# One gate block is moved from the third group's chain to the last group of a hybrid Conformer and RWKV-7 layer, and the norm's row sums refer to four blocks

## The chip, the cores and the metric

The kernel runs on one core of one Trainium2 chip. The metric is the device time of one execution in microseconds (us); less is better. A profile is one execution, and its span runs from the first to the last instruction. PE is TensorE, DVE VectorE, ACT ScalarE, POOL GpSimd, SP SyncE, which here issues nearly all the transfers.

## The reference

One layer on 512 tokens of width 1024, all in float32. From the modulated norm `h` one wide product gives the columns of a convolution branch, of an RWKV-7 branch and of two gates:

```python
h = modulate(rms_norm(x, g_norm1), shift1, scale1)
u = h @ w_in
u_conv, u_rwkv, u_gate = jnp.split(u, [2 * CONV_DIM, 2 * CONV_DIM + RWKV_COLS], axis=-1)
y_conv = conformer_conv(u_conv, ...)   # z*sigmoid, 31 taps, layer_norm, silu, z @ w_pw + b_pw
y_rwkv = rwkv7_mix(u_rwkv, ...)        # 16 heads of 64, a recurrence over 512 tokens, @ w_o
g_conv, g_rwkv = jnp.split(jax.nn.sigmoid(u_gate), N_BRANCH, axis=-1)
merged = g_conv * y_conv + g_rwkv * y_rwkv
x = x + gate1[:, None, :] * (merged @ w_out)
h2 = modulate(rms_norm(x, g_norm2), shift2, scale2)
x = x + gate2[:, None, :] * (jnp.square(jax.nn.relu(h2 @ w_ff1)) @ w_ff2)
```

The gates have 2 x 1024 columns, that is 16 blocks of 128. They need only `h`, and their result is used only after both branches.

## The kernel before

Columns lie on partitions, tokens on the free axis, so a tile is 128 columns by 512 tokens. A dense product of one block of 128 output columns (`wload`, `wmul`, lines 211 to 231) loads 1024x128 weights by SP (512 KB), splits them on ACT into a rounded high part (line 215) and on POOL into the rest (line 216), and runs 3 x 8 matmuls of 128x512 (lines 223 to 225): high by high, high by low, low by high. Raw weights, high and low parts have two buffers each, so the weights of a block are made ready about two blocks ahead.

The RWKV branch goes in four groups of two column blocks (four heads). For a group: `group_k` (line 547) makes two key blocks (read by ACT at line 263) and the low-rank decay and rate; `group_prep` (593) makes two receptance and two value blocks and the pair products (line 664, masked by DVE at 667) of 8 chunks of 64 tokens; `group_solve` (705) inverts the triangular part on DVE in 62 small dependent steps (lines 722 and 724) between transposes (715, 730, 732); `group_solve2` (739) finishes this on PE (748, 754); `group_chain` (759) walks over the 8 chunks, each a chain of small matmuls with ACT and DVE between them; `group_post` (810) normalizes, and reads for each block a 64 KB weight g2t into a single buffer (833) for a product (835).

Blocks that depend on `h` alone fill PE beside this: six convolution blocks (`conv_in`, 514; the 31 taps are DVE steps at line 145; line 530 adds a block to the column sums `csum`) and the 16 gate blocks (`gate_in`, 848: the dense block, a sigmoid on ACT at line 850, a store at 851). `WINDOWS` says for each group which of them are traced ahead of its chain and, after the bar, behind it ("c" is a convolution block, "g" a gate block).

Instructions are traced in program order, and a scheduler orders each engine's queue from that: what is ready goes, by priority, which is the place in the program less an offset from the table `FORWARD`. `issue_after` and `amid` only add that an instruction stands behind a given other one on its engine. Each queue then runs strictly in its order on the chip.

The last group has the layer norm of the convolution in front of its chain (lines 888 to 909): mean by a matmul over `csum` (893), ACT's copy (895), eight tiles read back and the mean subtracted on POOL (903), squares on ACT (905), row sums on PE (`rms_rows`, 188), then root (198), reciprocal on DVE (199), a broadcast by PE (183) and a copy (909). The silu of the normed blocks (938 to 941) makes the input of the pointwise product `w_pw` (line 947), which then runs beside the last chain. The row sums of tile j are put behind a numbered matmul of the blocks just traced:

```python
steps = sum(dense_log[-lnb:], [])          # 24 matmuls of each of the last lnb blocks
with tc.issue_after(steps[min(NORM_AT + j * NORM_STEP, len(steps) - 1)].ins):   # 63, 9
    rms_rows(pq, sq, j == 0, j == KC - 1)
```

After the last chain's place in the program the rest of the gate blocks, the pointwise product, `w_o`, `w_out` and the feed-forward follow, all dense.

Of the kernel before, what the change touches and what calls it, by code (L numbers as in the profile page):

```python
# [19 lines left out]
NCH = 8  # L20
TAPS = 31

WINDOWS = ("ccgg|g", "ccggg|", "cc|gggg", "ggg|ggg")

FORWARD = {
    "k": (10, 10, 10, 10), "solve": (127, 153, 48, -153), "window": (0, 7, -47, -43), "chain": (-98, 348, 51, 37),
# [31 lines left out]
def tile_block(ctx: ExitStack, tc: tile.TileContext, xT, vec, cst, x0, w_ada, w_in, w2a2, g2w,  # L58
# [8 lines left out]
    def nm(s):  # L67
        cnt[0] += 1
        return f"{s}{cnt[0]}"

    @contextmanager
    def forward(section, g=0, shift=True):

        off = FORWARD[section][g]
        if not off:
            yield
            return
        with tc.high_priority(offset=off):
            a = tc.cur_priority
            yield  # L80
            n = tc.cur_priority - a
        if shift:
            tc.cur_priority += n
# [3 lines left out]
    def t2k(shape=(P, T), dt=F32, tag="t2k", bufs=9):  # L87
        home = sb if tag == "t2k" else pools["A2" if tag in A2 else "A"]
        return home.tile(list(shape), dt, name=nm(tag), tag=tag, bufs=bufs)
# [10 lines left out]
    def pmisc(shape=(P, T), name="misc"):  # L100
        return psum("misc", 2, shape, name)
# [83 lines left out]
    def rms_rows(pq, sq, start, stop):  # L185

        for q in range(4):
            pe.matmul(pq[32 * q:32 * q + 32, :], ones[:, 0:32], sq[:, q * P:(q + 1) * P], start=start, stop=stop,
                      tile_position=(0, 32 * q))
# [6 lines left out]
    def rms_tail(pq, ei):  # L196
        rt = sb.tile([P, P], F32, name=nm("nrm"), tag="nrm", bufs=1)
        act.activation(rt, pq, AF.Sqrt, scale=1.0 / D, bias=eps[:, ei:ei + 1])
        dve.reciprocal(rt, rt)
        pr = pmisc((P, T), "rmsb")  # L200
        bcast_rows(pr, rt)
        return pr
# [30 lines left out]
    def after_dense():  # L233

        return tc.issue_after(last[0].ins)

    @contextmanager
    def amid(n, d=-1):

        with forward("amid", shift=False), tc.issue_after(dense_log[d][n].ins):  # L240
            yield
# [455 lines left out]
    def group_bonus(g, G, b):  # L697
        rH, rL, v = G.bonus[b]
        pb = pmisc(name="bonus")
        pe.matmul(pb, blkr, rH, start=True, stop=False)  # L700
        pe.matmul(pb, blkr, rL, start=False, stop=True)
        dve.tensor_tensor(v, pb, v, ALU.mult)
        nc.sync.dma_start(vb_d[g * NB + b], v)

    def group_solve(G):


        U = NB * NCH
        AD = atile("s4", (P, 2, NB, NCH, 32), 2)
        for q in range(4):  # L710
            d, e = q % 2, 1 - q // 2
            for h in range(2):
                act.copy(AD[32 * q:32 * q + 32, h], G.G[32 * q:32 * q + 32, :, e, :, 32 * d:32 * d + 32])
        AT = atile("s4", (P, 32, 32), 2)
        dve.transpose(AT, AD.rearrange("p h b c t -> p t (h b c)"))
        X = psum("Y", 1, (P, 32, 16))
        act.copy(X, xi)
        tmp = atile("tm", (P, 144))
        for s in range(31):
            n, w = 31 - s, s // 2 + 1  # L720
            tv = tmp[:, 0:n * w].rearrange("p (t c) -> p t c", c=w)
            dve.tensor_tensor(tv, AT[:, s + 1:32, s].unsqueeze(2).to_broadcast([P, n, w]),  # L722
                              X[:, s, 0:w].unsqueeze(1).to_broadcast([P, n, w]), ALU.mult)
            dve.tensor_tensor(X[:, s + 1:32, 0:w], tv, X[:, s + 1:32, 0:w], ALU.add)  # L724
        Xf = atile("s4", (P, 32, 16, 2), 2)
        act.copy(Xf[:, :, :, 0], X)
        dve.stream_shuffle(Xf[:, :, :, 1], Xf[:, :, :, 0], [(i + 16) % 32 for i in range(32)])
        Xv = Xf.rearrange("p t c h -> p t (c h)")
        T1 = atile("s4", (P, 32, 32), 2)
        dve.transpose(T1.rearrange("p u c -> p c u"), Xv.rearrange("p t c -> p c t"))  # L730
        TT = atile("TT", (P, 32, 32))
        G.solved = dve.transpose(TT.rearrange("p u t -> p t u"), Xv)
        for q in range(4):
            d, e = q % 2, 1 - q // 2
            act.copy(G.G[32 * q:32 * q + 32, :, e, :, 32 * d:32 * d + 32],
                     TT[32 * q:32 * q + 32, 0:U, :].rearrange("p (b c) t -> p b c t", b=NB))
        G.T1, G.TT = T1, TT

    def group_solve2(G):
        U = NB * NCH  # L740
        T1, TT = G.T1, G.TT
        W = atile("s4", (P, U, 32), 2)
        pw = pmisc((P, U, 32), "sW")
        px = pmisc((P, NB, NCH, 32), "sX")
        los = ((0, 1), (64, 0))
        for u in range(U):
            for lo, e in los:
                pe.matmul(pw[lo + 32:lo + 64, u, :], G.G[lo:lo + 32, u // NCH, e, u % NCH, 32:64], T1[lo:lo + 32, u, :],
                          start=True, stop=True, tile_position=(lo, lo + 32))
        for lo, e in los:  # L750
            act.copy(W[lo + 32:lo + 64], pw[lo + 32:lo + 64])
        for u in range(U):
            for lo, e in los:
                pe.matmul(px[lo:lo + 32, u // NCH, u % NCH, :], W[lo + 32:lo + 64, u, :], TT[lo + 32:lo + 64, u, :],
                          start=True, stop=True, tile_position=(lo + 32, lo))
        for lo, e in los:
            act.copy(G.G[lo:lo + 32, :, e, :, 32:64], px[lo:lo + 32])
# [100 lines left out]
    def window(items):  # L858
        for kind in items:
            if kind == "g":  # L860
                gate_in(next(blocks_g))
                continue
            j = next(blocks_c)
            zs[j] = conv_in(j)
            if j < 4:
                conv_taps(j - 2, zs[j - 2])
            with tc.issue_after(G.solved.ins):
                conv_taps(j, zs[j])
# [8 lines left out]
    for g in range(4):  # L877
        with forward("solve", g):
            group_solve(G)
        win = WINDOWS[g].split("|")  # L880
        lnb = 3 if g == 3 else 1
        for i in range(lnb):
            with forward("window", g):
                window(win[0][i:i + 1])
            if i == 0:
                with after_dense():
                    group_bonus(g, G, 1)
        if g == 3:

            with forward("norm"):  # L890
                steps = sum(dense_log[-lnb:], [])
                pm = pmisc(name="mean")
                pe.matmul(pm, ones, csum, start=True, stop=True)
                mean = t2k()
                act.activation(mean, pm, AF.Copy, scale=1.0 / D)
                pq = pmisc((P, P))
                ct8 = []
                for j in range(KC):
                    ct8.append(t2k())
                    nc.sync.dma_start(ct8[j], conv_d[j])  # L900
                for j in range(KC):
                    t = ct8[j]
                    pool.tensor_tensor(t, t, mean, ALU.subtract)  # L903
                    sq = sb.tile([P, T], F32, name=nm("nsq"), tag="nsq", bufs=2)
                    act.activation(sq, t, AF.Square)
                    with tc.issue_after(steps[min(NORM_AT + j * NORM_STEP, len(steps) - 1)].ins):
                        rms_rows(pq, sq, j == 0, j == KC - 1)
                plr = sb.tile([P, T], F32, name=nm("nsq"), tag="nsq", bufs=2)
                act.copy(plr, rms_tail(pq, 1))
        with forward("window", g):  # L910
            window(win[0][lnb:])
        with amid(SOLVE_AT[g]):
            group_solve2(G)
        if g == 3:
            stA2.close()
        with forward("chain", g):
            Y = group_chain(G)
        if g == 3:
            break
        with forward("between", g):  # L920
            window(win[1])
        with forward("k", g + 1):
            Gn = group_k(g + 1)
        group_prep(g + 1, Gn)
        with forward("post", g):
            group_post(g, G, Y)
        G = Gn
# [244 lines left out]
```

## Time and profile before

| | us |
|---|---|
| median of 3 runs | 1128.13 (1125.83 to 1128.40) |
| the profiled execution | 1128.09 |
| its span | 1126.3 |
| PE busy, weight loads busy | 1063.0, 816.3 |
| DVE, ACT, POOL busy | 756.3, 487.9, 460.5 |

| stretch of the span, us | what runs |
|---|---|
| 0 to 75 | first norm, its modulation, first blocks |
| 75 to 540 | the groups, convolution and gate blocks |
| 540 to 582 | tail of the third group, layer norm, last solve |
| 582 to 640 | last chain beside the pointwise product |
| 640 to 1126 | `w_o`, `w_out`, feed-forward, last norm |

A row of a timeline gives the start, the duration, engine, line, operation, tiles (out<-in), shapes and count; in brackets how long the engine was idle before it and what ended that. A row of the groups by line gives the count, then busy us and mean ns, then idle us before them. A queue is written SPq. A row of the chain of waits gives start, duration and what it was.

### The profile page before, as it was taken

The page shows a single profiled execution, that of the slowest core. Times are in us where ns is not written, and L with a number is a line of the kernel's source. Part 1 is how long each engine was busy: PE and PEld are TensorE (multiplying, and loading weights), DVE is VectorE, ACT ScalarE, POOL GpSimd, SP SyncE. Part 2 cuts the span into 40 slices and gives each one's busy share as a digit, 9 for nine tenths or more (in the row PEclk, how much of TensorE's full clock was granted, in tenths as well). Part 3 has the DMA queues.
Part 4 walks back from the last instruction along what each step waited for, and adds up shares of the span by engine and source line. Part 5 has one row for each costly group of instructions (what it writes and reads, how often), then busy time and mean ns, then how long its engine had stood idle before and what let it go on. Part 6 is the DMA issues. An engine that isn't in the chain of part 4 may idle for free.

```text
span 1126.3 us, 16021 instructions
## 1 busy us (share of the span) xinstructions
PE 1063.0 (94%) x6290; PEld 816.3 (72%) x6290; DVE 756.3 (67%) x1133; ACT 487.9 (43%) x794; POOL 460.5 (41%) x265
## 2 busy tenths in 40 slices
PE   6989899999999999999769999998999999999996
PEld 5766686677866677677445788876888888888885
DVE  5878887789878998679766757879413513512555
ACT  5557445547355654646363323335313312322431
POOL 4745442264424443443501244453444444444441
PEclk9989899899999999999968999999999999999999
DMA  9712242111521134022636689942333333333332
GB/s 318 228 42 84 61 127 76 52 57 59 179 87 52 39 105 153 20 67 84 214 118 215 217 281 298 290 131 57 94 96 103 101 94 94 94 94 96 104 99 77
DMA packets 188922, 136.73 MB, mean 121 GB/s; under 512 B 5424, under 2 KB 162480, under 8 KB 188848
## 3 DMA queue, kind: packets, MB, share of 16 engines
q1 hardware_dynamic: 188848, 135.73, 39.3%
q8 instruction: 49, 0.80, 0.3%
q14 instruction: 25, 0.20, 0.1%
HBM read 121.55 MB, written 14.16 MB: 120 GB/s over the span
## 4 chain that ended last, share of the span: by engine, by line
PE 71%; DVE 15%; ACT 5%; DMA 3%; POOL 3%; issue 2%; SPq 0%; DVEq 0%; ACTq 0%; POOLq 0%
PE mm L224 18%; PE mm L223 18%; PE mm L225 18%; DVE acc L145 2%; PE pG L664 2%; PE Y L802 1%; PE Y L800 1%; ACT wH L215 1%; POOL wL L216 1%; PE ch L768 1%; PE ch L777 1%; DVE t2k L251 1%; PE ch L785 1%; DVE t2k L1023 1%; POOL t2k L903 1%
## 5 line engine op out<-in xcount | busy, mean ns | idle before, releaser
L216 POOL TENSOR_TENSOR wL<-raw,wH 128x1024 fp32r<-128x1024 f32 x142 | 341.1, 2402 | 535.3 <-ACT wH L215 488.5
L225 PE MATMUL mm<-b,wL 128*128 128x512 f32 x720 | 289.6, 402 | 2.4 <-POOL wL L216 2.3
L224 PE MATMUL mm<-b,wH 128*128 128x512 f32 x720 | 289.0, 401 | 2.1 <-DVE b L1033 2.0
L223 PE MATMUL mm<-b,wH 128*128 128x512 f32 x720 | 289.7, 403 | 0.0
L215 ACT CAST wH<-raw 128x1024 fp32r<-128x1024 f32 x142 | 149.2, 1050 | 289.8 <-PE mm L224 246.3
L145 DVE SCALAR_TENSOR_TENSOR acc<-z,vt,acc 128x512 f32<-128x512 f32 x232 | 173.2, 746 | 1.6
L225 PEld LDWEIGHTS mm<-b,wL 128*128 128x128 f32 x720 | 135.9, 189 | 34.7 <-POOL wL L216 4.7
L224 PEld LDWEIGHTS mm<-b,wH 128*128 128x128 f32 x720 | 136.0, 189 | 33.2 <-DVE b L1033 3.4
L223 PEld LDWEIGHTS mm<-b,wH 128*128 128x128 f32 x720 | 136.0, 189 | 30.5 <-issue 3.2
L224 PE MATMUL mm<-g,wH 128*128 128x512 f32 x328 | 128.2, 391 | 1.1 <-DVE g L1025 0.9
L223 PE MATMUL mm<-g,wH 128*128 128x512 f32 x328 | 128.5, 392 | 0.0
L225 PE MATMUL mm<-g,wL 128*128 128x512 f32 x328 | 127.8, 390 | 0.0
L1023 DVE TENSOR_TENSOR t2k<-t2k 128x512 f32<-128x512 f32 x32 | 72.9, 2284 | 57.8 <-ACT t2k L1020 57.5
L1067 DVE SCALAR_TENSOR_TENSOR x<-mm,cols,x 128x512 f32<-128x512 f32 x31 | 23.3, 751 | 114.4 <-PE mm L225 114.4
L224 PEld LDWEIGHTS mm<-g,wH 128*128 128x128 f32 x328 | 61.6, 188 | 15.3 <-DVE g L1025 2.2
L223 PEld LDWEIGHTS mm<-g,wH 128*128 128x128 f32 x328 | 61.6, 188 | 14.0 <-ACT g L1024 1.2
L225 PEld LDWEIGHTS mm<-g,wL 128*128 128x128 f32 x328 | 61.6, 188 | 13.0 <-issue 0.2
L1024 ACT CAST g<-t2k 128x512 fp32r<-128x512 f32 x32 | 19.8, 621 | 72.6 <-DVE t2k L1023 72.6
L1025 DVE TENSOR_TENSOR g<-t2k,g 128x512 fp32r<-128x512 f32 x32 | 23.4, 736 | 19.9 <-ACT g L1024 19.9
L724 DVE TENSOR_TENSOR Y<-tm,Y 128x126 f32<-128x126 f32 (+22 forms) x124 | 31.8, 257 | 3.3
L664 PEld LDWEIGHTS pG<-AR,BK 64*128 64x128 f32 x256 | 24.7, 189 | 12.1 <-DVE G L667 6.3
L722 DVE TENSOR_TENSOR tm<-s,Y 128x126 f32<-128x126 f32 (+22 forms) x124 | 31.0, 250 | 3.1
(291 smaller groups left out, 1563.1 us busy)
## 6 DMA issues: line engine op xcount, KB each, us to landing
raw<-in_w_ff_dram SPq DMA_DIRECT2D x64, 512.0 KB, 4.0
raw<-in_w_in_dram SPq DMA_DIRECT2D x54, 512.0 KB, 3.7
adaw<-in_w_ada_dram SPq DMA_DIRECT2D x10, 1024.0 KB, 6.7
t2k<-gate SPq DMA_DIRECT2D x24, 256.0 KB, 3.9
adac<-in_w_ada_dram SPq DMA_DIRECT2D x24, 256.0 KB, 3.3
wa<-in_w_ada_dram SPq DMA_DIRECT2D x11, 512.0 KB, 5.8
gate<-cv SPq DMA_DIRECT2D x16, 256.0 KB, 2.9
raw<-in_w_pw_dram SPq DMA_DIRECT2D x8, 512.0 KB, 4.5
```

The source lines that it names most:

```text
L145: dve.scalar_tensor_tensor(dst if i == n - 1 else so_far, row, col, so_far, ALU.mult, ALU.add)
L215: act.copy(wH, raw)
L216: last_low[0] = pool.tensor_tensor(wL, raw, wH, ALU.subtract)
L223: steps.append(pe.matmul(acc, wH[:, kc, :], aH(kc), start=kc == 0, stop=False))
L224: steps.append(pe.matmul(acc, wH[:, kc, :], aL(kc), start=False, stop=False))
L225: steps.append(pe.matmul(acc, wL[:, kc, :], aH(kc), start=False, stop=kc == KC - 1))
L664: pe.matmul(pgs[e][:, i, :], BK[64 * e:64 * e + 64, c, C * e:C * e + 2 * C], G.AR[64 * e:64 * e + 64, b, c, :], start=True, stop=True)
L722: dve.tensor_tensor(tv, AT[:, s + 1:32, s].unsqueeze(2).to_broadcast([P, n, w]), X[:, s, 0:w].unsqueeze(1).to_broadcast([P, n, w]), ALU.mult)
L724: dve.tensor_tensor(X[:, s + 1:32, 0:w], tv, X[:, s + 1:32, 0:w], ALU.add)
L1023: dve.tensor_tensor(t, t, t, ALU.mult)
L1025: dve.tensor_tensor(rL(f), t, rH(f), ALU.subtract)
L1067: dve.scalar_tensor_tensor(x1(j), acc, ada[:, 40 + j:41 + j], x1(j), ALU.mult, ALU.add)
```

## The change

Two numbers of the program. The third group's entry in `WINDOWS` has three gate blocks behind its chain instead of four; the last group's has four instead of three ahead of its chain, and still three behind. `lnb`, the number of blocks that are traced ahead of the norm in the last group, follows: 4 instead of 3. So `steps` has 96 entries instead of 72, and the row sums of tiles 0 to 7 stand behind entries 63, 72, 81, 90, 95, 95, 95, 95 instead of 63 and seven times 71. The number of gate blocks, their order and all arithmetic stay.

```diff
-WINDOWS = ("ccgg|g", "ccggg|", "cc|gggg", "ggg|ggg")
+WINDOWS = ("ccgg|g", "ccggg|", "cc|ggg", "gggg|ggg")
...
         win = WINDOWS[g].split("|")
-        lnb = 3 if g == 3 else 1
+        lnb = 4 if g == 3 else 1
         for i in range(lnb):
             with forward("window", g):
                 window(win[0][i:i + 1])
```

## Rows read from the trace of the kernel before

**Rows 1.** Page, part 1: busy time, share of the span, instructions.

```profile
PE 1063.0 (94%) x6290; PEld 816.3 (72%) x6290; DVE 756.3 (67%) x1133; ACT 487.9 (43%) x794; POOL 460.5 (41%) x265
```

**Rows 2.** Stage view: stretch, length, busy us of PE, PEld, DVE, ACT, POOL; clock.

```profile
322.68:380.50 57.82, 56.67 (x598) 38.67 (x598) 47.27 (x81) 36.09 (x75) 21.92 (x19) 1.00 0.16 47
440.66:504.27 63.61, 63.57 (x628) 43.21 (x628) 47.92 (x82) 38.46 (x77) 25.86 (x19) 1.00 0.17 49
...
558.00:582.00 24.00, 10.31 (x189) 7.69 (x188) 12.49 (x22) 15.06 (x24) 5.95 (x4) 0.57 0.22 69
800.00:900.00 100.00, 99.55 (x440) 81.65 (x440) 37.55 (x29) 29.05 (x38) 42.98 (x18) 1.00 0.33 94
```

**Rows 3.** Groups by line on PE, 322.68 to 380.50; L225 is like L224.

```profile
L224 PE MATMUL mm<-b,wH 128*128 128x512 f32 x33 | 13.9, 420 | 0.0
L223 PE MATMUL mm<-b,wH 128*128 128x512 f32 x32 | 13.5, 422 | 0.0
```

**Rows 4.** The same view, 440.66 to 504.27; its other two dense lines are alike.

```profile
L223 PE MATMUL mm<-b,wH 128*128 128x512 f32 x42 | 18.0, 429 | 0.0
```

**Rows 5.** Timeline of ACT: key blocks read (L263), gate sigmoids (L850).

```profile
315.99 0.68 ACT L263 ACTIVATE kk<-mm,cols 128x512 f32<-128x512 f32 x1
...
430.14 0.59 ACT L850 ACTIVATE cv<-mm 128x512 f32<-128x512 f32 x1
...
435.58 0.59 ACT L850 ACTIVATE cv<-mm 128x512 f32<-128x512 f32 x1
...
441.01 0.68 ACT L263 ACTIVATE kk<-mm,cols 128x512 f32<-128x512 f32 x1
...
453.31 0.69 ACT L263 ACTIVATE kk<-mm,cols 128x512 f32<-128x512 f32 x1
...
533.28 0.58 ACT L850 ACTIVATE cv<-mm 128x512 f32<-128x512 f32 x1
...
537.52 1.28 ACT L850 ACT_TABLE_LOAD   x1
```

**Rows 6.** Timelines of PE and DVE: where the solves of groups 2 and 3 end.

```profile
322.68 1.20 PE L748 MATMUL sW<-s,G 32*32 32x32 f32 x64 [1.16 <-DVE s L730]
...
438.35 2.21 DVE L730 STREAM_TRANSPOSE s<-s 128x1024 f32<-128x1024 f32 x1
...
440.62 1.20 PE L748 MATMUL sW<-s,G 32*32 32x32 f32 x64
```

**Rows 7.** The chain of waits, 534 to 583.

```profile
536.45 1.06 ACT wH L215
...
537.58 2.62 POOL wL L216
540.22 0.38 SPq L213
540.64 3.82 DMA g2t<-in_g2w_dram
...
544.60 1.10 PE g L835 x2
...
546.86 0.87 PE mean L893 x2
...
559.16 2.34 POOL wL L216
...
582.27 1.15 PE mm L223 x2
```

**Rows 8.** Timeline of DVE: the last add to the column sums, the norm's reciprocal.

```profile
534.78 0.68 DVE L530 TENSOR_TENSOR csum<-csum,co 128x512 f32<-128x512 f32 x1
...
566.33 0.95 DVE L199 RECIPROCAL nrm<-nrm 128x128 f32<-128x128 f32 x1 [7.53 <-ACT nrm L198]
```

**Rows 9.** Timeline of PE: the first and the last of eight row-sum steps.

```profile
553.74 0.43 PE L188 MATMUL misc<-nsq,ones 128*32 128x128 f32 x8 [1.45 <-ACT nsq L905]
...
564.67 0.66 PE L188 MATMUL misc<-nsq,ones 128*32 128x128 f32 x8 [0.58 <-ACT nsq L905]
```

## The prediction

> **What bounds the kernel now.** I read the busy line of the page first, then busy time by stage, then the chain of waits, then single rows. TensorE (PE) is busy 94% of the span and nothing else is over 67% [rows 1], so the question is where PE is *not* full. The stage view answers it: in the third group's chain (440.66 to 504.27) PE has 63.57 of 63.61 us, but from 558 to 582 it has 10.31 of 24.00, at a granted clock of 0.57, which is a mixture of the two levels, 1.2 and 2.4 GHz [rows 2]. So 13.7 us of PE time lie idle in front of the first matmul of the pointwise product. Total PE work does not change with this edit. It can only gain if what ends that hole comes sooner, or lose if it comes later.
>
> What ends the hole is the chain of waits [rows 7]: the last gate weights are cast on ACT (536.45) and subtracted on POOL (537.58), this frees a raw buffer for which SP's queue waits (540.22), behind it stands the load of g2t (540.64), for g2t waits a matmul of the previous group's tail (544.60), and behind that in PE's queue stands the mean (546.86). Then come POOL's subtractions with two weight subtractions among them (the second at 559.16), the reciprocal (566.33), and at 582.27 the first pointwise matmul. The column sums that the mean reads start their last add on VectorE (DVE) at 534.78 and take 0.68 us [rows 8], so the mean starts 11.4 us after its data is there.
>
> **The change, part by part.** *1. The block leaves the third group.* A gate block is 24 matmuls; two gate sigmoids in a row start at 430.14 and 435.58, so a block is 5.44 us of PE time when PE does nothing else [rows 5]. The four run one behind the other up to 435.58, under the third group's solve. The solve ends on DVE: its first transpose runs 438.35 to 440.56, and PE starts the step that reads it at 440.62 [rows 6]. DVE sets that moment, so taking PE work away in front of it does not move it. What it moves is the work behind the gates in PE's order: the two key blocks of the next group. Now their results are read at 441.01 and 453.31, at and behind the solve's end [rows 5]. With one block fewer ahead, the second key block ends 5.44 us sooner in PE's order and lies almost wholly under the solve, and the chain of the third group is left with one block fewer between its steps.
>
> Is that worth anything? Group 2 shows it (its solve ends at 322.68). There no gate follows the chain, and the second key block is read at 315.99, before the solve's end [rows 5, 6]. From the solve's end to the first pair product of the next group it takes 57.82 us and holds 33+33+32 = 98 dense matmuls [rows 2, 3]; the same stretch of the third group takes 63.61 us and holds 3 x 42 = 126 [rows 2, 4]. DVE does the same work in both (47.27 against 47.92 us [rows 2]). So 28 dense matmuls fewer go with 5.79 us less, 0.207 us each, and 24 fewer are worth 24 x 0.207 = 5.0 us. Upper end: 5.44 us, the block at its full rate. Lower end: 0, if PE's order pulls other ready blocks between the chain's steps (the next group's gates are ready all the time). I take 5.0, because group 2 is the same stage and its gates were as ready, and yet it ran with 98.
>
> The stage's matmul column is full, its weight loads are not: 43.21 of 63.61 us, 68%, against 81.65 of 100 in the dense stretch 800 to 900 [rows 2]. So the chain's own latency could be the limit there, with the dense matmuls lying in its gaps for nothing (rival B). The two groups speak against that: both have 67 to 68% weight loads and yet differ in length by the time of the dense matmuls [rows 2 to 4]. The Trainium skill (Perfetto Trace Analysis, section Identifying the Most-Contended Engine) says that matmul busy time is no good measure of how full TensorE is, and that the busy share of the weight loads is to be taken instead; going by it, PE has a third of the stage to spare and the sum would be 1128.1 instead of 1123.1.
>
> *2. What goes with the block.* One 512 KB weight load and one gate store on SP, one cast (1.06 us) and one sigmoid (0.59) on ACT, one subtraction (about 2.4) on POOL [rows 5, 7]. In the third group they hide under the solve and leave nothing behind. In the last group they come back: seven weight sets instead of six.
>
> *3. The block comes back before the norm.* The last group now has four blocks ahead of its chain and three behind. Counted over all groups the block that the norm's steps refer to is the thirteenth gate block in both versions (9+4, before 10+3), so its place on PE's clock stays. PE work up to the hole is the same; the block fills time that the earlier chain set free. Cost on PE: 0. On POOL and ACT the price depends on how many weight sets fall between the mean and the last subtraction. Now it is two, some 2.4 us each (the second 2.34 [rows 7]). With the norm 5 us earlier against an unchanged sequence of blocks it may be one (-2.4) or, with one set more in the group, three (+2.4). I take 0 between these ends.
>
> *4. The row sums.* Before, the eight row-sum steps stand behind matmuls 63, 71, 71, ... of three blocks; now behind 63, 72, 81, 90, 95, ... of four. The thirteenth gate's sigmoid starts at 533.28 [rows 5], and the row sums run at 553.74 to 564.67, each released by ACT's square [rows 9]. The places named are passed 20 us before the data is there, so this part costs and gives 0. Bounds: no gain, since squares release them, and at most the 0.66 us of one step [rows 9] where it now stands behind a matmul of the fourth block.
>
> *5. What is late next.* If products, solve and sums of the last group start 5.0 us sooner, the mean is next: it moves only if g2t moves too. The tail of the third group moves with its chain, so the load's place in SP's queue should fall one weight load earlier. DVE waits 7.53 us in front of the reciprocal with the last solve steps behind it [rows 8]; both sides move together, so I leave that wait as it is.
>
> Sum, against the profiled execution (1128.09 us, span 1126.3; it lies within 0.04 of the median 1128.13): 1128.1 - 5.0 + 0 + 0 = **1123.1 us**. The known bounds of this case alone: 1128.1 - 5.44 - 2.4 = 1120.3 to 1128.1 - 5.0 + 2.4 = 1125.5.
>
> **The rivals.** *A: the mean stays where it is.* The raw load at 540.22 is held by POOL's subtraction for the sixteenth gate, and the sequence of gate blocks does not move on the clock. If the order on SP keeps g2t behind this load, the mean stays at 546.9 and the hole ends at 582: 1128.1. For it: the chain of waits runs just there [rows 7]. Against it: the tail's matmul itself is issued with the third group's chain, which would be 5 us earlier.
>
> *B: the chain's latency sets the third group's stage.* Then fewer matmuls between its steps leave PE idle there and nothing starts sooner: 1128.1. For it: the 68% of part 1. Against it: group 2 [rows 3, 4].
>
> *C: slower, the seventh weight set stands in the norm's way.* Place: POOL and ACT between the mean and the last square. If a third set falls there and the mean does not move, POOL adds 2.4, ACT a cast and a sigmoid (1.06 + 0.59) and a table load (1.28, as at 537.52) [rows 5, 7]: 5.3 us, so 1133.4. It decides from the point where three weight subtractions, not two, lie between the mean and the last norm subtraction, with the chain of group 3 no shorter. For it: two are there already. Against it: the norm would have to stay while the group in front of it has less to do.
>
> *D: the reciprocal's wait opens.* The order on DVE is worked out anew. If the last solve steps come before the reciprocal, the solve ends up to 7.5 us sooner [rows 8], on top of 5.0: 1115.6.
>
> *E: the change does not do what it says.* For the row sums I hold this to be so (part 4); it has no time of its own.
>
> **How the numbers follow.** Forecast 0.42, D 0.08, A 0.20, B 0.08, C 0.22; E holds in all of them. About 0.3% (3.4 us) is what a measurement of this kernel can tell from no change. The forecast and D are beyond it on the fast side, A and B are within it, C is beyond it on the other: faster 0.50, same 0.28, slower 0.22. The forecast's own range is 1120.3 to 1125.5; with D's end below and C's above it is 1116 to 1133.5.
>
> **What would show it.** Right: the second key block read before 447, not at 453; solve end to first pair product of the third group at 58 to 59 us with about 100 dense matmuls; the mean near 542; first pointwise matmul near 577; PE idle before it smaller by about 5 us. Part 3: count of weight subtractions between mean and last norm subtraction. Part 4: row sums still released by squares. The prediction is wrong if that stretch still holds some 126 dense matmuls (other blocks were pulled in), or if it shrinks but g2t still lands near 544.5 (rival A), or if the order of work elsewhere changes so that PE is idle where it is full now.

## The result, and the profile after

The kernel after takes 1134.55 us (median of 5 runs, 1133.62 to 1141.42) against 1128.40 for the kernel before beside it: a ratio of 1.0073 [1.0044, 1.0102]. It is 0.7% slower, where 1123.1 us had been forecast, and it lies above the range.

The page of after, part 1 (busy us, share of the span, instructions), against [rows 1], shows the same work:

```profile
span 1137.1 us, 16021 instructions
...
PE 1067.6 (94%) x6290; PEld 817.7 (72%) x6290; DVE 756.2 (67%) x1133; ACT 488.5 (43%) x795; POOL 459.8 (40%) x265
```

In this profiled execution (1139.11 us) TensorE's granted clock fell behind the third group's solve, which it did not in another execution of the same order (last section). I therefore read the changed kernel from e2 below and the kernel before from e1: e2 has the order of after on every engine, e1 that of before, and in neither did the clock fall there. The stage view of e2: the third group's stage, and the stretch from the mean to the first pointwise matmul (columns as in [rows 2]):

```profile
439.42:502.92 63.50, 63.13 (x622) 42.52 (x622) 47.34 (x81) 36.54 (x75) 23.45 (x18) 1.00 0.16 47
542.36:582.64 40.28, 22.35 (x247) 14.17 (x245) 22.82 (x62) 24.56 (x35) 14.56 (x10) 0.69 0.45 144
```

The first line answers [rows 2]: the stage that should have come down to 58 us takes 63.50, as before. In the stretch of the second line PE is idle for 17.9 us; in e1 the same stretch is 35.49 us long, with 15.6 idle. The stage's groups by line on PE, against [rows 4], say why it did not shrink:

```profile
L223 PE MATMUL mm<-b,wH 128*128 128x512 f32 x41 | 17.7, 432 | 0.0
L225 PE MATMUL mm<-b,wL 128*128 128x512 f32 x41 | 17.3, 422 | 0.0
```

The third dense line (L224) has 40, so there are 122 dense matmuls where 126 stood. The key blocks did slip under the solve (ACT reads them at 432.51 and 437.96, in before at 441.01 and 453.31 [rows 5]), but the last group's own gates took their place: 24 matmuls of its first gate and 7 of its second.

The loss is further on. DVE's timeline around the norm's reciprocal (start, us, engine, line, operation, tiles, count, wait before it and what ended it), e1 first, as in [rows 8]:

```profile
564.71 0.95 DVE L199 RECIPROCAL nrm<-nrm 128x128 f32<-128x128 f32 x1 [7.52 <-ACT nrm L198]
565.57 0.17 DVE L724 TENSOR_TENSOR Y<-tm,Y 128x30 f32<-128x30 f32 x1
565.78 0.17 DVE L722 TENSOR_TENSOR tm<-s,Y 128x16 f32<-128x16 f32 x1
565.99 0.18 DVE L724 TENSOR_TENSOR Y<-tm,Y 128x16 f32<-128x16 f32 x1
...
566.86 1.28 DVE L727 STREAM_SHUFFLE s<-s 128x512 f32<-128x512 f32 x1
568.57 0.69 DVE L938 TENSOR_TENSOR t2k<-t2k,nsq 128x512 f32<-128x512 f32 x1 [0.43 <-ACT nsq L909]
569.18 2.00 DVE L730 STREAM_TRANSPOSE s<-s 128x1024 f32<-128x1024 f32 x1
571.04 1.93 DVE L732 STREAM_TRANSPOSE TT<-s 128x1024 f32<-128x1024 f32 x1
572.79 4.29 DVE L938 TENSOR_TENSOR t2k<-t2k,nsq 128x512 f32<-128x512 f32 x7
```

and e2, the order of after:

```profile
563.71 0.95 DVE L199 RECIPROCAL nrm<-nrm 128x128 f32<-128x128 f32 x1 [9.41 <-ACT nrm L198]
564.58 0.21 DVE L724 TENSOR_TENSOR Y<-tm,Y 128x70 f32<-128x70 f32 x1
...
567.44 0.69 DVE L938 TENSOR_TENSOR t2k<-t2k,nsq 128x512 f32<-128x512 f32 x1 [1.21 <-ACT nsq L909]
...
568.13 0.68 DVE L938 TENSOR_TENSOR t2k<-t2k,nsq 128x512 f32<-128x512 f32 x1
...
568.81 2.49 DVE L938 TENSOR_TENSOR t2k<-t2k,nsq 128x512 f32<-128x512 f32 x4
...
571.23 1.29 DVE L727 STREAM_SHUFFLE s<-s 128x512 f32<-128x512 f32 x1
572.32 0.71 DVE L938 TENSOR_TENSOR t2k<-t2k,nsq 128x512 f32<-128x512 f32 x1
572.95 2.00 DVE L730 STREAM_TRANSPOSE s<-s 128x1024 f32<-128x1024 f32 x1
574.86 1.88 DVE L732 STREAM_TRANSPOSE TT<-s 128x1024 f32<-128x1024 f32 x1
```

The last group's solve ends with the transpose L732. In before it starts 6.33 us behind the reciprocal, with three steps of the solve (L722, L724) and one of the norm's eight silu products (L938) between; in after 11.15 us, with nine steps and seven products between, the first of which waits 1.21 us for the normaliser's copy on ACT. PE, which needs the transposes for the last chain, stands idle for it; its timeline, e1:

```profile
571.33 1.92 PE L748 MATMUL sW<-s,G 32*32 32x32 f32 x64 [3.54 <-DVE s L730]
```

and e2:

```profile
575.10 1.92 PE L748 MATMUL sW<-s,G 32*32 32x32 f32 x64 [8.44 <-DVE s L730]
```

### The profile page after: what moved, and what is told of

It is laid out like the page before. It is cut to its first block, busy times and chain, and to the rows that moved or that the text cites. A ratio compares the mean times of both kernels' runs of the same rounds, so it can differ in the third digit from the quotient of the medians.

```text
span 1137.1 us, 16021 instructions
## 1 busy us (share of the span) xinstructions
PE 1067.6 (94%) x6290; PEld 817.7 (72%) x6290; DVE 756.2 (67%) x1133; ACT 488.5 (43%) x795; POOL 459.8 (40%) x265
## 4 chain that ended last, share of the span: by engine, by line
PE 42%; DVE 5%; ACT 2%; DMA 2%; POOL 1%; issue 1%; DVEq 0%; ACTq 0%; SPq 0%; POOLq 0%
PE mm L224 13%; PE mm L223 13%; PE mm L225 12%; DMA raw<-in_w_o_dram 1%; DVE t2k L1023 1%; ACT wH L215 1%; DVE b L1033 1%; PE misc L169 1%; POOL wL L216 1%; PE mm L1081 0%; DMA t2k<-conv 0%; PE Y L802 0%; DVE t2k L251 0%; DVE t2k L1103 0%; PE Y L800 0%
## 5 line engine op out<-in xcount | busy, mean ns | idle before, releaser
L225 PE MATMUL mm<-b,wL 128*128 128x512 f32 x720 | 290.7, 404 | 3.4 <-POOL wL L216 3.3
L224 PE MATMUL mm<-b,wH 128*128 128x512 f32 x720 | 291.5, 405 | 2.1 <-DVE b L1033 2.0
L225 PEld LDWEIGHTS mm<-b,wL 128*128 128x128 f32 x720 | 136.9, 190 | 35.6 <-POOL wL L216 5.5
L224 PEld LDWEIGHTS mm<-b,wH 128*128 128x128 f32 x720 | 137.2, 191 | 34.5 <-issue 3.7
L224 PE MATMUL mm<-g,wH 128*128 128x512 f32 x328 | 128.3, 391 | 1.1 <-DVE g L1025 0.9
L225 PE MATMUL mm<-g,wL 128*128 128x512 f32 x328 | 127.8, 390 | 0.0
L224 PEld LDWEIGHTS mm<-g,wH 128*128 128x128 f32 x328 | 61.6, 188 | 15.3 <-DVE g L1025 2.2
L225 PEld LDWEIGHTS mm<-g,wL 128*128 128x128 f32 x328 | 61.6, 188 | 12.9 <-issue 0.2
L664 PE MATMUL pG<-AR,BK 64*128 64x128 f32 x256 | 29.2, 288 | 5.2 <-DVE G L667 3.4
L724 DVE TENSOR_TENSOR Y<-tm,Y 128x126 f32<-128x126 f32 (+22 forms) x124 | 31.8, 256 | 3.3
```

Of the source, the lines that this page charges most:

```text
L224: steps.append(pe.matmul(acc, wH[:, kc, :], aL(kc), start=False, stop=False))
L225: steps.append(pe.matmul(acc, wL[:, kc, :], aH(kc), start=False, stop=kc == KC - 1))
L664: pe.matmul(pgs[e][:, i, :], BK[64 * e:64 * e + 64, c, C * e:C * e + 2 * C], G.AR[64 * e:64 * e + 64, b, c, :], start=True, stop=True)
```

## The experiments

Executions of one order differ by some microseconds upstream of all this, so the table counts from the first transpose (L715) of the third group's solve: at 401.85 in e1, 400.41 in e2. Columns: that solve, from L715 to its L730; dense matmuls in the stage behind it, and its length (solve end to first pair product); start of the reciprocal; start of the last solve's final transpose, and how far behind the reciprocal; the last chain's last read of a first product (L773, ACT); end of the span. All are in us. The last columns are the median and the ratio to the kernel before run beside it (its medians were 1127.17 for e1 to e4, 1128.14 for e5 to e8, 1127.46 for e9 to e11).

| run | solve | dense, stage | recip. | transpose (behind) | last read | end | median | ratio |
|---|---|---|---|---|---|---|---|---|
| e1 (order of before) | 34.81 | 126, 63.61 | 162.86 | 169.19 (6.33) | 222.95 | 722.9 | 1127.21 | 1.0003 [0.9973, 1.0032] |
| e2 (order of after) | 36.81 | 122, 63.50 | 163.30 | 174.45 (11.15) | 229.52 | 729.7 | 1133.58 | 1.0060 [1.0029, 1.0091] |
| e3 | 36.65 | 122, 63.51 | 171.16 | 169.44 (-1.72) | 224.71 | 731.1 | 1133.34 | 1.0049 [1.0020, 1.0077] |
| e4 | 35.11 | 126, 63.62 | 169.11 | 167.39 (-1.72) | 222.72 | 727.8 | 1129.65 | 1.0011 [0.9982, 1.0040] |
| e5 | 36.84 | 122, 63.52 | 163.54 | 170.95 (7.41) | 220.82 | 723.0 | 1127.18 | 0.9998 [0.9969, 1.0028] |
| e6 | 34.80 | 125, 64.18 | 162.72 | 173.06 (10.34) | 230.33 | 729.8 | 1133.57 | 1.0035 [1.0002, 1.0068] |
| e7 | 34.71 | 125, 64.18 | 162.11 | 169.25 (7.14) | 219.29 | 721.9 | 1128.31 | 0.9995 [0.9966, 1.0023] |
| e8 | 36.86 | 91, 60.60 | 169.06 | 173.26 (4.20) | 223.40 | 724.3 | 1126.80 | 0.9980 [0.9952, 1.0009] |
| e9 | 34.75 | 126, 63.59 | 164.65 | 175.24 (10.59) | 230.80 | 730.5 | 1133.48 | 1.0038 [1.0006, 1.0071] |
| e10 | 36.78 | 115, 62.86 | 167.58 | 171.71 (4.13) | 220.50 | 723.1 | 1126.94 | 0.9998 [0.9969, 1.0027] |
| e11 | 34.72 | 118, 63.58 | 167.20 | 171.36 (4.16) | 220.66 | 721.9 | 1127.27 | 0.9990 [0.9958, 1.0022] |

**e1: the row sums alone**, on before.

```diff
-                steps = sum(dense_log[-lnb:], [])
+                steps = sum(dense_log[-4:], [])
```

> The kernel before with only the row sums spread: they refer to the last four blocks traced (entries 63, 72, 81, 90, 95, ...), and no gate block is moved. If the spread costs time: about +6 us against before. If the spread is empty, as part 4 of the prediction has it: equal to before within 2 us, with the row sums still released by ACT's squares, the mean near 547 and the reciprocal with three solve steps behind it on DVE.

The order on every engine stayed that of before, and so did the time. Part 4 and rival E hold: the spread does nothing.

**e2: the block alone**, on after, with the row sums spread over three blocks.

```diff
-                steps = sum(dense_log[-lnb:], [])
+                steps = sum(dense_log[-3:], [])
```

> The kernel after with the row sums put back to the places of before (last three blocks, entries 63 and 71); only the gate block is moved. If the move carries the loss: about +6 us against before, with the third group's solve end to first pair product at 64 us or more and some 122 dense matmuls in it. If the spread carries it: equal to before. Second question, for the granted clock: the profile after showed half clock from 440 to about 454, behind a wait of 1.1 us for the solve; if that belongs to the order of work it stands here too, if it was chance it is gone and the stage is some 5 us shorter.

The order is that of after, and 1.0060 is within after's interval: the whole loss is in the moved block.

**e3: after, with the reciprocal held behind the solve; e4: the same on before.**

```diff
-        dve.reciprocal(rt, rt)
+        with tc.issue_after(behind.ins) if behind is not None else ExitStack():
+            dve.reciprocal(rt, rt)
...
-                act.copy(plr, rms_tail(pq, 1))
+                act.copy(plr, rms_tail(pq, 1, G.solved))
```

> The kernel after with the norm's reciprocal put behind the last solve's final transpose on DVE, nothing else. Theory 1 (the loss lies in DVE's order: eight solve steps, six silu products and the transposes stand behind a reciprocal that waits 9.7 us): the last solve ends near 565 instead of 582, the first pointwise matmul comes 5 to 8 us sooner, the time falls to 1127 to 1130. Rival (the loss lies in the third group's stage and in what follows from it, the sums and the mean): the norm's path to the reciprocal stays as it is, the first pointwise matmul moves by under 2 us, the time stays at 1133 to 1135.

> The kernel before with the same edit of DVE's order. Three solve steps and the transposes stood behind the reciprocal, which waited 7.5 us. Theory 1: the last solve ends near 562 instead of 572.8, the gain is smaller than in the kernel after, 1 to 5 us, since the norm's root and broadcast still have to come: 1123 to 1127. Rival: same as before within 2 us, since the silu path ends the hole alone.

My first theory (the steps that stand behind the reciprocal are the loss) fell in this form. In e3 the solve's last transpose came 5.0 us sooner and the chain's last read 4.8, but the reciprocal came 7.9 us later, all silu products behind it, and the end stayed. In e4's profile the reciprocal came 6.3 us later and the end 4.9, though the chain's last read stayed (222.72); its timed ratio can't be told from 1. So the end seems to wait for both: the chain, and the norm's products. The clock is a rival for a part of it. Stage views of e1, e3 and e4, in this order:

```profile
585.00:600.00 15.00, 15.00 (x130) 9.60 (x132) 9.28 (x18) 9.88 (x21) 0.18 (x1) 1.00 0.65 204
...
585.00:600.00 15.00, 15.00 (x108) 9.48 (x107) 7.78 (x16) 9.26 (x20) 0.00 (x0) 0.72 0.56 178
...
585.00:600.00 15.00, 15.00 (x95) 9.80 (x94) 6.88 (x15) 7.80 (x16) 0.00 (x0) 0.72 0.55 171
```

With the products late, TensorE's granted clock rose late too, and PE got through 108 and 95 matmuls there where e1 had 130. No run here separates the products from the clock.

**e5: after, with only the silu products held behind the solve.** The reciprocal stays where it is.

```diff
-            dve.tensor_tensor(t, t, plr, ALU.mult)
+            with tc.issue_after(G.solved.ins):
+                dve.tensor_tensor(t, t, plr, ALU.mult)
```

> The kernel after, with the eight silu products of the norm (DVE, 0.43 to 0.6 us each) held on DVE's queue behind the last solve's final transpose; nothing else moves on DVE up to the reciprocal (it still stands ahead of the last eight solve steps). Theory 2, the loss is made on DVE between the reciprocal and the last solve's transpose, where seven silu products, one of them waiting for the normaliser's copy, stand in the solve's way: the transpose comes 3 to 5 us sooner after the reciprocal (about 7 us behind it instead of 11), the last group's chain starts as much sooner, and the time is 1129 to 1131. Theory 3, what is lost there is not what the end waits for, the silu products are needed as soon as the solve is: the first pointwise matmul comes later by what the chain gains, and the time stays at 1133 to 1135.

The transpose comes 7.41 us behind the reciprocal, and the whole loss is gone: 1127.18, better than my 1129 to 1131. Nine solve steps still stand behind the reciprocal, and a wait of 1.30 us for ACT behind them (0.69 in e1), which leaves 1.1 us more than in e1. The stage of the third group is as it was (122 matmuls, 63.52 us). Held back, the products also turned PE's order. The groups by line on PE from the first product with the chain's state (L768) to the last read, e2:

```profile
L225 PE MATMUL mm<-c,wL 128*128 128x512 f32 x28 | 12.2, 436 | 0.0
L224 PE MATMUL mm<-c,wH 128*128 128x512 f32 x28 | 12.0, 430 | 0.0
L223 PE MATMUL mm<-c,wH 128*128 128x512 f32 x26 | 11.0, 422 | 0.0
```

and e5:

```profile
L225 PE MATMUL mm<-c,wL 128*128 128x512 f32 x23 | 10.4, 451 | 0.0
L224 PE MATMUL mm<-c,wH 128*128 128x512 f32 x23 | 10.2, 452 | 0.0
L223 PE MATMUL mm<-c,wH 128*128 128x512 f32 x22 | 9.5, 438 | 0.0
```

There are 68 pointwise matmuls between the chain's steps where 82 stood, and this part of the chain takes 37.6 us instead of 41.3. So of the 8.7 us by which the last read comes sooner, 3.5 are the transpose, 3.7 lie there and 1.5 between the two. I take the 14 matmuls for the cause of the 3.7, but it is only argued. e1 has 69 of them and yet took 42.2 us, but in its profile the clock fell in this part:

```profile
611.00:617.00 6.00, 6.00 (x36) 3.67 (x35) 1.94 (x6) 0.99 (x3) 0.00 (x0) 0.50 0.94 297
```

e10 below has 69 too; its clock did not fall again in this part, which took 36.9 us.

**e6: after, with the DVE step of the last group's key blocks held behind the third solve; e7: e5 and e6 together.**

```diff
+    def shifted(acc, dst, j, ahead=0, behind=None):
...
+        with forward("shift") if ahead else tc.issue_after(behind.ins) if behind is not None else ExitStack():
...
+            Gn = group_k(g + 1, G.solved if g == 2 else None)
```

> The kernel after, with the DVE step of the last group's two key blocks held behind the third group's solve, as it stood in the kernel before. Theory 4, that step inside the solve (0.75 us, and 1.32 us of waiting for ACT) is the 1.9 us by which the third solve became longer: the solve takes 34.8 us instead of 36.7 from its transpose to its last one, the stage behind it is unchanged at 63 to 64 us (125 dense matmuls in it instead of 122), and the time falls by 1 to 2 us to 1132. Rival: the wait moves to the key block's next reader and the stage becomes longer by what the solve gains, so 1133 to 1135.

> The two holds together. If theories 2 and 4 hold and the two places are in series on one path, the gains add: 1127 to 1129, the time of the kernel before. If only theory 2 holds, 1129 to 1131; if both fall, 1133 to 1135. Nothing in either theory takes it below 1126, since the stage behind the third solve still has 125 dense matmuls as it had before.

In after this step stands among the solve's steps, and the solve waits with it for ACT; DVE's timeline of e2:

```profile
433.22 0.75 DVE L265 SCALAR_TENSOR_TENSOR kk<-mm,vt,kk 128x511 f32<-128x511 f32 x1 [1.32 <-ACT kk L263]
```

Held back, the solve is 2.0 us shorter (34.80), as expected, but the stage is 0.7 longer and the time did not move in e6, nor in e7 against e5, nor in e11 against e10. That a change under 0.3% lies in it can't be excluded.

**e8: after, with the matmuls of the last group's four window gates held behind its first pair product.**

```diff
-        act.activation(t, w_in_block(GT0 + j * P), AF.Sigmoid)
+        w = wload(w_in, 0, GT0 + j * P)
+        with tc.issue_after(behind.ins) if behind is not None else ExitStack():
+            acc = wmul(w, hH, hL)
+        act.activation(t, acc, AF.Sigmoid)
...
-                window(win[0][i:i + 1])
+                window(win[0][i:i + 1], G.pair if g == 3 else None)
```

> The kernel after, with the matmuls of the last group's four window gates held behind its first pair product, so that the planner can't pull them into the third group's chain: 91 dense matmuls stand between the third solve's second part and that product, where 122 stood. This asks what a dense matmul there is worth. Theory by the prediction's price (0.207 us each, the stage bound by what PE has queued): the stage goes from 63.5 us to 63.5 - 31 x 0.207 = 57.1 us. Rival, the chain's own latency sets the stage: it stays at 62 to 64 us. The two blocks come back later, ahead of the mean or behind it, so the time is 1127 to 1131 by the first and 1133 to 1136 by the second.

The size is neither theory's: 31 dense matmuls fewer made the stage 2.9 us shorter, 0.094 each, half of the price that group 2 had suggested. The clock fell near the end of this stage (last section), so this price alone would be unsure; but 7 fewer without a fall gave 0.64 us in e10 against e2 and 0.60 in e11 against e6, 0.09 each. In place of the rest PE waits for the chain, which it hardly does with 122 in the stage (0.37 us idle in e2); PE's timeline of e8, all waits in the stage:

```profile
492.33 0.33 PE L804 MATMUL Y<-UV,G 128*64 128x64 f32 x2 [0.41 <-ACT UV L781]
494.72 0.34 PE L770 MATMUL ch<-S,AR 64*64 64x64 f32 x4 [1.38 <-DVE S L795]
496.21 0.54 PE L802 MATMUL Y<-Sd,AR 128*64 128x128 f32 x2 [0.79 <-ACT Sd L809]
497.73 0.68 PE L804 MATMUL Y<-UV,G 128*64 128x64 f32 x3 [0.36 <-ACT UV L781]
501.27 1.02 PE L664 MATMUL pG<-AR,BK 64*128 64x128 f32 x6 [1.61 <-DVE AR L641]
```

They sum to 4.55 us. The time fell all the same to 1126.80. I take the reason to be that of e5, though the shorter stage may have a part in it: with the gates held, the planner put the solve's steps ahead of the reciprocal and the products behind the two transposes, which now start 2.22 and 4.20 us behind the reciprocal.

**e9: before, with the silu products' priority on DVE raised**, so that all eight stand ahead of the two transposes. No block moves.

```diff
-            dve.tensor_tensor(t, t, plr, ALU.mult)
+            with tc.high_priority(offset=700):
+                dve.tensor_tensor(t, t, plr, ALU.mult)
```

> The kernel before, with only the priority of the norm's eight silu products on DVE raised, so that all eight stand ahead of the last solve's two final transposes, as seven do in the kernel after. Every block stands where it stood. Theory 2, these products are the loss: the final transpose comes 3 to 4 us later behind the reciprocal (10 us instead of 6.3), the last group's chain and the end as much, and the time goes from 1127 or 1128 to 1131 or 1133. Rival, the moved block itself makes the loss and the order on DVE only came with it: the time stays within 2 us of before.

DVE's timeline of e9:

```profile
574.03 0.95 DVE L199 RECIPROCAL nrm<-nrm 128x128 f32<-128x128 f32 x1 [8.72 <-ACT nrm L198]
...
577.89 4.91 DVE L939 TENSOR_TENSOR t2k<-t2k,nsq 128x512 f32<-128x512 f32 x8 [0.43 <-ACT nsq L909]
582.71 2.06 DVE L730 STREAM_TRANSPOSE s<-s 128x1024 f32<-128x1024 f32 x1
584.62 1.92 DVE L732 STREAM_TRANSPOSE TT<-s 128x1024 f32<-128x1024 f32 x1
```

The transpose comes 10.59 us behind the reciprocal and the median is 1133.48, that of after; the ratio, 1.0038, is above 1 with its whole interval. So the loss can be made in before by raising these products alone, as e5 takes it out of after by holding them alone. Up to the products every engine has the order of e1 (in e5, of e2); behind them the planner sorted PE's queue anew as well, in e9 to the 82 pointwise matmuls beside the chain that e2 has (41.8 us), in e5 to 68. What the two runs show is thus the place of the products with what follows from it.

**e10: after, with gates two to four held as in e8; e11: e10 with the hold of e6.** Of these gates only 7 matmuls had stood ahead of the pair product.

```diff
-                window(win[0][i:i + 1])
+                window(win[0][i:i + 1], G.pair if g == 3 and i >= 1 else None)
```

> The kernel after, with the last three of the last group's four window gates held behind its first pair product; the first gate's 24 matmuls stay in the third group's chain and 7 of the second leave it (115 dense matmuls in the stage instead of 122). With it the planner puts the last solve's steps ahead of the reciprocal and the silu products behind its transposes, of itself. Theory 2: the final transpose comes 4 us behind the reciprocal instead of 11, and the time is that of before or under it, 1125 to 1128; the stage of the third chain is shorter by 7 x 0.1 to 7 x 0.207 us, 0.7 to 1.4. Rival: the seven matmuls, held, come late ahead of the mean and the time is 1130 or more.

> The kernel of the run before this one, with the key blocks' DVE step held behind the third solve too (solve of 34.8 us instead of 36.8). If the third solve is on the path of the end, 1.5 to 2 us less than that run, 1123 to 1126, which would be under the kernel before; if the two microseconds are lost again in the last chain, as in the earlier run with this hold alone (its time did not move), the same time within 1 us.

With those gates held the planner's order on DVE turns (transpose 4.13 us behind the reciprocal) and the time is that of before. No version beats before: in e5, e7 and e10 the last chain's last read is 2.1 to 3.7 us sooner than in e1, but the end lies between 0.3 us later and 0.9 sooner. Around the chain's end PE has hardly a gap left; stage view, e10:

```profile
600.00:650.00 50.00, 49.79 (x355) 36.30 (x355) 34.51 (x55) 19.09 (x36) 14.29 (x6) 1.00 0.73 236
```

In e1 PE had 47.48 of these 50 us. Of the 2.3 us won there a part is lost again behind: from 640 to 700 PE is busy 58.20 us in e10 and 59.26 in e1. Where the rest goes was not followed up.

## Why the prediction was wrong

- **Part 1 failed, in three places.** The gain was 0, the lower end that I had named (ready gates pulled into the chain) and set aside, because group 2 had run with 98: 122 matmuls, 63.50 us. That DVE sets the solve's end was right, but I overlooked that the key blocks bring a DVE step of their own, which now stands in the solve (36.81 us for 34.81). And 0.207 us a matmul was mis-sized: taken out without replacement they gave 0.09 (e8, e10, e11). Group 2 and group 3 differ in more than their dense matmuls.
- **Rival B** was half right. The matmul column of the stage was full, but taking a quarter of its dense matmuls out opened 4.55 us of waiting for the chain. The Trainium skill (Perfetto Trace Analysis, section Identifying the Most-Contended Engine) had said not to read matmul busy time as fullness; e8 bears this out in part: under a full matmul column lay 4.55 us of waits, but the stage did become 2.9 us shorter.
- **Part 4 held, parts 2 and 3 within their bounds.** The mean comes 1.3 us sooner in e2 than in e1 (141.95 for 143.23, the table's count) and the reciprocal 0.4 later, so the norm between them takes 1.7 us more where I had put 0. The extra time is on ACT. In e1 the cast of the next weights runs among the norm's squares (L905), at 555.71; in e2 it waits for a matmul and stands between the last square and the root:

```profile
559.51 0.63 ACT L905 ACTIVATE nsq<-t2k 128x512 f32<-128x512 f32 x1 [0.50 <-POOL t2k L903]
560.95 1.04 ACT L215 CAST wH<-raw 128x1024 fp32r<-128x1024 f32 x1 [0.81 <-PE mm L224]
562.01 1.28 ACT L198 ACT_TABLE_LOAD   x1
```

It is not what the end waits for: e5 has the reciprocal as late (163.54) and no loss.

- **Rival C** had nearly the measured time (1133.4), but that was luck: between mean and last norm subtraction stands one weight subtraction, not three, and the mean did move. **Rival A** fell too, but the mean moved by 1.3 us only, not by 5.
- **Part 5 is the step that cost the time.** I left the reciprocal's wait as it was, since both sides would move together, and took the order behind it as given. The wait grew by 1.9 us (9.41 for 7.52), but the loss lies in what stands behind it. Rival D named this place ("the order on DVE is worked out anew") but only with a better order. It came out worse: six more products and six more solve steps between the reciprocal and the final transpose, 5.3 us on the final one, 6.6 on the chain's last read, 6.8 on the end. So the 5.0 us of part 1 did not come, and about 6 were lost here (6.0 in e9's median), which gives 1134. e5 and e9 show the place of the products, with what follows from it, to be the cause; e10 shows that holding gates two to four back turns it. How the planner's reckoning comes to it was not looked at. The granted clock is a rival for a part of the 6 us: it rose later in e2 than in e1 (0.62 against 1.00 from 585 to 590). Its late rise is not needed for the loss: e6, which has the loss, shows 0.89 from 585 to 595, and e5, which has not, the same 0.89 from 586.77 to 596.77. But in e6 it fell once more (0.66 from 604 to 614), so the clock's part stays open.

## What to carry to other kernels

Where a planner orders the queues, moving one block re-sorts the engines that did not look involved, so list what stands behind every long wait in a shared queue, and price each with the worse of its orders too. If short steps of two consumers stand behind one wait, hold the ones that the longer chain does not need. Do not rely on a price per matmul that comes from comparing two stages until matmuls are taken out and the stage is seen to shrink: here it was twice too high.

## What the runs showed of the hardware

The granted clock can fall in one execution and not in another of the same order of work, behind the same wait. PE had waited 1.14 us (after) and 1.15 us (e2) for the third solve just ahead of these two stretches. Stage view of after:

```profile
440.00:450.00 10.00, 9.93 (x141) 6.65 (x141) 7.50 (x10) 5.46 (x9) 1.16 (x1) 0.57 0.19 54
450.00:460.00 10.00, 10.00 (x64) 6.12 (x64) 4.18 (x9) 3.97 (x9) 1.63 (x1) 0.75 0.00 1
```

and of e2:

```profile
440.00:450.00 10.00, 10.00 (x148) 6.75 (x140) 8.45 (x13) 6.72 (x13) 0.50 (x1) 1.00 0.19 54
450.00:460.00 10.00, 10.00 (x99) 6.03 (x98) 7.72 (x15) 8.28 (x16) 2.37 (x1) 1.00 0.20 56
```

That stage took 69.28 us in after and 63.50 in e2, so one profile would have blamed it on the change. In e8 the clock fell behind the first three of the waits listed above, 2.58 us in all, and then stood at the lower level, 1.2 GHz, for 16 us, in which the other two lie:

```profile
497.00:513.00 16.00, 14.03 (x70) 11.06 (x67) 10.87 (x18) 1.86 (x5) 1.28 (x1) 0.50 0.04 12
```

The dense matmuls just ahead of the wait in after start 0.23 us apart, those behind it at the lower level 0.43 us. By these, the 14.03 us of busy PE above would have taken some 7.5 us at the full clock (an estimate). So the waits that a lighter stage opens can cost more than their length.
